# State-space layer: two heads side by side in the array, decay rows and sample rows laid out on 128 rows, state times C in four quarters

## The chip, the cores and the metric

One Trainium2 chip, one core. The metric is the device time of one execution in microseconds, the median of three runs. All matrices lie in HBM as float32. The engines are TensorE (PE in the profile; PEld is its weight load), VectorE (DVE), ScalarE (ACT), GpSimd (POOL) and SyncE (SP), which issues the DMAs.

## The reference, cut to what matters

Four decoder layers (retention, state space, gated delta net, retention), each with a token mixer and an MLP, run over a prompt of 256 tokens and 8 samples of 4 tokens with the same weights: T = 288 columns in the kernel. The state-space mixer (32 heads of width 64, 8 groups of 4 heads, state width 128) is where most of the change lies:

```python
def _ssd(h, conv_buf, s0, w_in, conv_w, conv_b, dt_bias, a_log, d_skip, norm_w, w_out):
    z, xbc, dt = jnp.split(h @ w_in, [...], axis=-1)
    xbc, new_buf = _causal_conv(xbc, conv_buf, conv_w)
    xs, b_in, c_out = jnp.split(jax.nn.silu(xbc + conv_b), [...], axis=-1)
    dt = jax.nn.softplus(dt + dt_bias)
    log_a = dt * (-jnp.exp(a_log))
    y, s_new = _decay_scan(c_out, b_in, xs * dt[..., None], log_a, s0g)
    y = y + d_skip * xs
    ...
def _decay_scan(q, k, v, log_a, s0):
    ct = jnp.cumsum(log_a)
    decay = jnp.where(incl, jnp.exp(ct[..., :, None] - ct[..., None, :]), 0.0)
    scores = jnp.einsum('bctgn,bcsgn->bcgts', qc, kc)
    y_intra = jnp.einsum('bcgrts,bcsgrp->bctgrp', scores[:, :, :, None] * decay, vc)
    y_inter = jnp.einsum('btgn,bgrnp,bgrt->btgrp', q_c, S, jnp.exp(ct_c))
    S = S * jnp.exp(ct_c[..., -1]) + jnp.einsum('bsgn,bgrs,bsgrp->bgrnp', k_c, w_end, v_c)
```

`y_inter` of the samples is state times C: each of the 8 samples has a state of its own for each head. The retention and delta-net mixers use the same idea of a decay per head; their outputs are normed per token and head and turned back into the layout of features on rows.

## The kernel before, in words

Activations lie as features on 128 partitions by 288 columns. Every dense product (`dense`, lines 192 to 225) splits the weights and the activations into two float32r parts and runs three matmuls for each 128x128 weight tile and 288 columns (L222, L223, L224, into `psd`): 12,336 of the 16,248 matmuls. The weights come by DMA into `raw`, ScalarE casts them (`wh`, L207) and VectorE makes the rest (`wl`, L210).

A mixer is worked in four units (`units`, m = 0 to 3; in the state-space layer a unit is two groups, g = 0 and 1, of four heads each). Within a unit a generator, the chain (`scan` in the retention and state-space layers, `prep` and `loop` in the delta net), yields estimated waits in us, and `weave` fills each wait with blocks of dense products: the unit's gate, the projection of the next unit and the output product of an earlier one. `fin` of unit m-1 runs ahead of the chain of unit m. The Tile framework then orders each engine's instructions by its own estimates. Each engine works its list in order. PSUM tiles come from `self.ps`: tag "m" has three banks, tag "s" two.

In a state-space unit `scan` does the following:

- State times C (L1090 to L1109): for each group, 8 samples' states `S` are transposed two samples at a time on TensorE (`ps_sT`), copied by ScalarE (`sT`, two buffers), and each sample's masked C (`cm`, 32 columns) is multiplied with it into `yi`. The output block of a matmul is 32 rows: sample b of a pair goes to rows 32*(2*g+b), so group 0 uses rows 0 to 63 and group 1 rows 64 to 127, with 256 columns. The products of four pairs are summed in each block.
- The states are updated (`ps_up`, L1111 to L1128) and stored; `yis` (L1132) is `yi` scaled by the decay of each token, group by group.
- For each of the eight heads, in four pairs: a matmul spreads the head's cumulative decay over 128 rows (`ps_cbc`, L1142). Its operands are `e2`, a column of ones at two places, and `cts`, the decays as a high part on rows 0 to 31 and a remainder on rows 32 to 63: 64 rows contracted. ScalarE makes the decay factors (`Et`, three buffers, L1147 to L1149), VectorE multiplies them with the scores `gm` (L1151). Then come the head's two products, 256 and 128 columns, into 64 rows of `y` (64*r for head r of the pair, L1155 and L1156). After both heads: one matmul adds `yis` (64 rows contracted, both heads' 128 outputs), two add the samples' own part (`xds`, 32 rows contracted). All lines of the local helper `mm` have line 983 in the profile.

In the retention layers `fin` (L748) transposes `yt` back: for each of four blocks two full 128x128 transposes and one of the 32 sample rows (L756). In the delta net `prep` spreads decays in the same way from 64 rows (`ps_dif`, L1354), and `fin` (L1696) transposes, for each of four heads, two prompt blocks (L1702, L1703) and 32 rows of `on2`, the samples' result (L1704). `on2` is written in two halves of 64 rows by `sample` (L1586): heads 0 and 1 first, heads 2 and 3 later.

Of the kernel before, what the change touches and what calls it, by code (L numbers as in the profile page):

```python
# [35 lines left out]
def make_consts():  # L36
# [50 lines left out]
    gm[:, 128:160] = np.tile(c["ssd_tris"][:, 0:32], (4, 1))  # L87
# [36 lines left out]
class K:  # L124
# [422 lines left out]
    def retention(self, ctx, j, i):  # L547
# [61 lines left out]
        def scan(h):  # L609
# [138 lines left out]
        def fin(h, ah, al):  # L748
            u = units.pop(h)
            yt, sgs = u["yt"], u["sg"]  # L750
            for z in range(4):
# [4 lines left out]
                nc.tensor.transpose(ps[:, 256:288], yt[:32, 2, zs], self.ident[:32, :32])  # L756
# [164 lines left out]
    def ssd(self, ctx, j, i):  # L921
# [15 lines left out]
        e2 = cp.tile([64, 32], F32R, name="e2")  # L937
# [9 lines left out]
        A.copy(e2, istk[0:64])  # L947
# [26 lines left out]
        la = rp.tile([128, 3, 2, 32], F32, name="la")  # L974
        for d in range(2):
# [32 lines left out]
        mm(ps[:64, 0:128], la2[:, 0], tri)  # L1008
        mm(ps[:64, 128:256], la2[:, 1], tri)
        mm(ps[:64, 256:288], la2[0:32, 2], tris[:, 0:32])  # L1010
        cth = rp.tile([64, T], F32R, name="cth")
        cts = rp.tile([64, T], F32R, name="cts")
        A.copy(cth, ps[:64, 0:T])
        V.scalar_tensor_tensor(out=cts, in0=cth, scalar=self.sel[:64, 0:1], in1=ps[:64, 0:T], op0=ALU.mult, op1=ALU.add)
# [13 lines left out]
        def scan(m):  # L1028
# [61 lines left out]
            for g in range(2):  # L1090
# [8 lines left out]
                for bp in range(4):  # L1099
                    ps = self.ps("ps_sT", "s")  # L1100
                    for b in range(2):
                        for q in range(2):
                            PE.transpose(ps[:, (2 * b + q) * 128:(2 * b + q + 1) * 128], S[q][:, 2 * bp + b], self.ident)
                    sT = rp.tile([128, 2, 256], F32, name="sT", tag="sT", bufs=2)
                    A.copy(sT.rearrange("p a b -> p (a b)"), ps)
                    for b in range(2):
# [22 lines left out]
            yis = rp.tile([128, 256], F32, name="yis", tag="yis")  # L1129
            for g in range(2):  # L1130
# [671 lines left out]
```

## Time and profile before

| | us |
|---|---|
| median of three runs | 2324.92 (2324.84 to 2326.75) |
| the profiled execution's own time | 2332.37 |
| its span, first to last instruction | 2330.2 |
| PE busy / DVE busy / ACT busy / POOL busy | 2241.3 / 1565.0 / 1245.0 / 574.3 |
| mean granted TensorE clock | 0.965 of 2.4 GHz |
| HBM traffic | 394.87 MB, 169 GB/s |

The span divides as follows: retention to about 290 us, its MLP to 570, the state-space layer to 900, its MLP to 1150, the delta net to 1550, its MLP to 1780, the second retention to 2100, the last MLP to the end. A busy time of PE counts matmuls whose ends are modelled and that overlap in the array, so the distance from one matmul's start to the next one's start says what a matmul costs. Times in a timeline are us from the span's start. A tile's form such as `64*128` is the rows and columns of the array that a matmul uses, and what follows is its output. A float32 matmul runs as two passes, so one matmul of the program shows as x2; a float32r one and a transpose run as one.

### The profile page before, as it was taken

What the parts mean: (1) busy time and instruction counts of PE and PEld (TensorE: products, weight loads), DVE (VectorE), ACT (ScalarE), POOL (GpSimd) and SP (SyncE); (2) the same over time, 40 slices, a digit from 0 to 9 for tenths busy, and PEclk for the clock granted to TensorE, in tenths of its full rate; (3) what the DMA queues carried; (4) which work ended last, traced back from release to release, by engine and by line L of the source; (5) the groups of instructions that cost most, each with busy time, mean ns of one, the idle gap of its engine ahead of it and who ended that gap; (6) DMA issues with size and microseconds to landing.
All of it is one profiled execution on the core that took longest, in us unless ns stands there. A gap on an engine that the chain in (4) does not pass through costs nothing. (4 is left out here: it accounts for less than half of the span.)

```text
span 2330.2 us, 42937 instructions
## 1 busy us (share of the span) xinstructions
PE 2241.3 (96%) x16248; PEld 2045.3 (88%) x16248; DVE 1565.0 (67%) x3209; ACT 1245.0 (53%) x2825; POOL 574.3 (25%) x597
## 2 busy tenths in 40 slices
PE   9999997998999999999899999999999999999998
PEld 8888797998888888999888888789899888879998
DVE  6777774557887777555786685557675777766554
ACT  5444463544667665555466566366655444445454
POOL 2110012332331222333332121124443001003333
PEclk9999998999999999999899998789999999999999
DMA  6786754545445543554433342247865666754553
GB/s 202 262 260 220 239 162 136 169 151 156 125 132 173 165 134 112 180 169 155 146 120 98 108 129 85 84 122 220 253 206 166 211 238 222 262 208 154 168 166 111
DMA packets 406656, 394.87 MB, mean 169 GB/s; under 512 B 15569, under 2 KB 356154, under 8 KB 406354
## 3 DMA queue, kind: packets, MB, share of 16 engines
q1 hardware_dynamic: 406290, 391.88, 53.2%
q8 instruction: 127, 2.08, 0.4%
q14 instruction: 79, 0.65, 0.1%
q10 hardware_dynamic: 96, 0.20, 0.0%
q0 software_dynamic: 64, 0.07, 0.0%
HBM read 333.41 MB, written 58.69 MB: 168 GB/s over the span
## 5 line engine op out<-in xcount | busy, mean ns | idle before, releaser
L207 ACT CAST wh<-raw 128x512 fp32r<-128x512 f32 x1024 | 627.0, 619 | 706.8 <-PE psd L223 649.3
L210 DVE TENSOR_TENSOR wl<-raw,wh 128x512 fp32r<-128x512 f32 x1024 | 741.6, 731 | 334.9 <-ACT wh L207 320.2
L222 PE MATMUL psd<-xh,wh 128*128 128x288 f32 x2576 | 782.1, 304 | 6.6 <-ACT xh L297 4.6
L223 PE MATMUL psd<-xl,wh 128*128 128x288 f32 x2576 | 776.2, 302 | 3.0 <-DVE xl L298 2.4
L224 PE MATMUL psd<-xh,wl 128*128 128x288 f32 x2576 | 774.4, 301 | 3.3 <-DVE wl L210 3.2
L222 PEld LDWEIGHTS psd<-xh,wh 128*128 128x128 f32 x2576 | 490.3, 191 | 28.7 <-issue 10.7
L223 PEld LDWEIGHTS psd<-xl,wh 128*128 128x128 f32 x2576 | 493.9, 192 | 19.2 <-issue 9.8
L224 PEld LDWEIGHTS psd<-xh,wl 128*128 128x128 f32 x2576 | 492.8, 191 | 13.5 <-DVE wl L210 5.6
L222 PE MATMUL psd<-ah,wh 128*128 128x288 f32 x1536 | 466.9, 304 | 24.5 <-ACT wh L207 11.3
L224 PE MATMUL psd<-ah,wl 128*128 128x288 f32 x1536 | 463.2, 302 | 4.2 <-DVE wl L210 4.1
L223 PE MATMUL psd<-al,wh 128*128 128x288 f32 x1536 | 463.9, 302 | 0.0
L222 PEld LDWEIGHTS psd<-ah,wh 128*128 128x128 f32 x1536 | 295.3, 192 | 35.5 <-ACT wh L207 19.5
L224 PEld LDWEIGHTS psd<-ah,wl 128*128 128x128 f32 x1536 | 296.6, 193 | 10.4 <-DVE wl L210 6.0
L223 PEld LDWEIGHTS psd<-al,wh 128*128 128x128 f32 x1536 | 296.1, 193 | 8.4 <-issue 6.5
L482 POOL TENSOR_TENSOR x<-x,dn 128x288 f32<-128x288 f32 x120 | 149.1, 1243 | 250.2 <-DVE dn L480 250.2
L463 POOL TENSOR_TENSOR a<-v 128x288 f32<-128x288 f32 x128 | 108.9, 851 | 271.9 <-ACT v L462 267.2
L725 DVE SCALAR_TENSOR_TENSOR S<-S,ps_up 128x512 f32<-128x512 f32 x128 | 83.4, 684 | 58.5 <-PE ps_up L724 49.9
L826 DVE SCALAR_TENSOR_TENSOR cacc<-U,cw,cacc 128x312 f32<-128x312 f32 x192 | 105.0, 552 | 10.1 <-ACT cacc L821 8.1
L465 DVE TENSOR_TENSOR al<-a,ah 128x288 fp32r<-128x288 f32 x128 | 59.4, 464 | 73.5 <-POOL a L463 69.4
L263 POOL TENSOR_TENSOR rs_y<-ms,mhalf 128x3 f32<-128x3 f32 (+3 forms) x37 | 36.5, 989 | 292.2 <-DVE ms L741 226.9
L802 POOL COPY U<-cb 128x24 f32<-128x24 f32 x64 | 35.0, 552 | 224.4 <-DVE cacc L826 106.7
L480 DVE TENSOR_TENSOR dn<-psd,rb 128x288 f32<-128x288 f32 x128 | 58.2, 454 | 40.5 <-PE psd L224 40.4
(498 smaller groups left out, 2658.6 us busy)
## 6 DMA issues: line engine op xcount, KB each, us to landing
raw<-mlp_w_up SPq DMA_DIRECT2D x64, 1024.0 KB
raw<-mlp_w_down SPq DMA_DIRECT2D x64, 1024.0 KB
S<-state_ret SPq DMA_DIRECT2D x64, 512.0 KB
raw<-ret_w_in SPq DMA_DIRECT2D x32, 1024.0 KB
s_ret<-S SPq DMA_DIRECT2D x64, 512.0 KB
raw<-ssd_w_in SPq DMA_DIRECT2D x24, 1024.0 KB
raw<-gdn_w_in SPq DMA_DIRECT2D x24, 1024.0 KB
raw<-ret_w_in SPq DMA_DIRECT2D x32, 512.0 KB
```

Of the source, the lines that this page charges most:

```text
L207: self.last_cast = nc.scalar.copy(wh, src)
L210: nc.vector.tensor_tensor(out=wl, in0=src, in1=wh, op=ALU.subtract)
L222: nc.tensor.matmul(po, lhsT=hs[k][:, os], rhs=xh[k], start=(k == 0), stop=False)
L223: nc.tensor.matmul(po, lhsT=hs[k][:, os], rhs=xl[k], start=False, stop=False)
L224: self.last_mm = nc.tensor.matmul(po, lhsT=ls[k][:, os], rhs=xh[k], start=False, stop=(k == kt - 1))
L263: self.nc.gpsimd.tensor_tensor(out=y[rows], in0=ms[rows], in1=self.mhalf[rows].broadcast_to([rows.stop - rows.start, n]), op=ALU.pow)
L463: nc.gpsimd.tensor_tensor(out=a, in0=v, in1=v, op=ALU.mult)
L465: nc.vector.tensor_tensor(out=al[o], in0=a, in1=ah[o], op=ALU.subtract)
L480: nc.vector.tensor_tensor(out=t, in0=ps, in1=rb2, op=ALU.mult)
L482: e.tensor_tensor(out=self.x[o], in0=self.x[o], in1=t, op=ALU.add)
L725: nc.vector.scalar_tensor_tensor(out=S[:, b, z], in0=S[:, b, z], scalar=C["g4"][h], in1=up, op0=ALU.mult, op1=ALU.add)
L826: nc.vector.scalar_tensor_tensor(out=acc[:, 0:n], in0=u, scalar=wk, in1=acc[:, 0:n], op0=ALU.mult, op1=ALU.add)
```

## The change

It changes seven things.

1. `e2`, `la`, `cts` and `cth` of the state-space layer have four copies on 128 rows where two lay on 64. `e2` is halved, so that the sum is the same. The matmul `ps_cbc` now contracts 128 rows.
2. The same for `gd`, `e2`, `cth` and `cts` of the delta net (`ps_dif`).
3. State times C runs on four samples at a time: sample b of four goes to rows 32*b, group g to columns 256*g. Two pairs are transposed and copied, then four matmuls follow. Each block sums two products.
4. `yis` is one VectorE instruction on 128x512 in place of two on 64x256, and the four row blocks are summed in the last matmul, which contracts 128 rows with four stacked identities.
5. The samples' own part contracts 128 rows: the tokens lie on the rows four times already, and the mask is divided by 4.
6. A pair's decays (`decays(pr)`) are issued one pair ahead of its products, `Et` has four buffers, and the products of the two heads alternate: 256 columns of both, 128 columns of both, the samples' part of both, the states' part of both.
7. The sample transposes at the end of retention (L756) and of the delta net (L1704) become matmuls over all 128 rows with 32 columns of the identity. In retention GpSimd clears the tile's third block first.

```diff
-    gm[:, 128:160] = np.tile(c["ssd_tris"][:, 0:32], (4, 1))
+    gm[:, 128:160] = np.tile(c["ssd_tris"][:, 0:32], (4, 1)) / 4.0
...
+            nc.gpsimd.memset(yt[:, 2], 0.0)
...
-                nc.tensor.transpose(ps[:, 256:288], yt[:32, 2, zs], self.ident[:32, :32])
+                nc.tensor.matmul(ps[:, 256:288], lhsT=yt[:, 2, zs], rhs=self.ident[:, :32], start=True, stop=True)
...
-        A.copy(e2, istk[0:64])
+        A.mul(e2, istk, 0.5)
...
-        for d in range(2):
+        for d in range(4):
             V.tensor_tensor(out=la[:, :, d], in0=dt, in1=bcm(nea, 3), op=ALU.mult)
...
-                for bp in range(4):
...
-                    for b in range(2):
-                        c = 32 * (2 * g + b)
-                        PE.matmul(yi[c:c + 32, 0:256], lhsT=cm[:, 2 * bp + b], rhs=sT[:, b], start=bp == 0, stop=bp == 3)
-                    yield YS[2]
+                for bq in range(2):
+                    sTs = []
+                    for bp in (2 * bq, 2 * bq + 1):
...
+                    yield 2 * YS[2]
+                    for b in range(4):
+                        PE.matmul(yi[32 * b:32 * b + 32, 256 * g:256 * g + 256], lhsT=cm[:, 4 * bq + b],
+                                  rhs=sTs[b // 2][:, b % 2], start=bq == 0, stop=bq == 1)
...
+            yv = []
+            P = decays(0)
+            yield YS[4]
+            for pr in range(4):
+                nxt = decays(pr + 1) if pr < 3 else None
+                if nxt:
+                    yield YS[4]
+
+                y = self.ps("ps_y")
+                hd = [(y[64 * r:64 * r + 64], slice(64 * (2 * pr + r), 64 * (2 * pr + r) + 64), P[r]) for r in range(2)]
+                for ys, cs, p in hd:
+                    mm(ys[:, 0:256], xdt[:, 0, cs], p[:, 160:416], True, False)
+                for ys, cs, p in hd:
+                    mm(ys[:, 128:256], xdt[:, 1, cs], p[:, 0:128], False, True)
+                for ys, cs, p in hd:
+                    mm(ys[:, 256:288], xds[:, cs], p[:, 128:160], True, False)
+                for ys, cs, p in hd:
+                    mm(ys[:, 256:288], yis[:, cs], istk, False, True)
...
-                PE.transpose(ps[:, 256:288], on[2][hp], ident[hp, hp])
+                PE.matmul(ps[:, 256:288], lhsT=on[2], rhs=ident[:, hp], start=True, stop=True)
```

The order of TensorE's list moves at three places that matter. In the rows a line number of the changed kernel is higher by the lines added above it (L984 is the helper L983, L1713 is L1704).

First, a pair of heads in the first state-space unit, before (`psd` is a dense product, its numbers tell tiles apart):

```order
L983 MATMUL ps_cbc<-cts,e_4177 128x288
L224 MATMUL psd<-xh_6834,wl 128x288
L983 MATMUL ps_y<-Et,xdt 64x256
L983 MATMUL ps_y<-Et,xdt 64x128
L222 MATMUL psd<-xh_6840,wh 128x288
L223 MATMUL psd<-xl_6841,wh 128x288
L983 MATMUL ps_y<-Et,xdt 64x256
L983 MATMUL ps_y<-Et,xdt 64x128
L983 MATMUL ps_y<-c_ssd_istk,yis 128x32
L983 MATMUL ps_y<-Et,xds 64x32 x2
```

and a pair of the same unit in the changed kernel:

```order
L222 MATMUL psd<-xh_6864,wh 128x288
L223 MATMUL psd<-xl_6865,wh 128x288
L224 MATMUL psd<-xh_6864,wl 128x288
L984 MATMUL ps_y<-Et,xdt 64x256 x2
L984 MATMUL ps_y<-Et,xdt 64x128 x2
L984 MATMUL ps_y<-Et,xds 64x32 x2
L984 MATMUL ps_y<-c_ssd_istk,yis 64x32 x2
L222 MATMUL psd<-xh_6822,wh 128x288
```

Dense products stood between the two heads of the pair; now both heads' products follow each other, the samples' parts too.

Second, a pair in the fourth unit of the changed kernel:

```order
L984 MATMUL ps_y<-Et,xdt 64x256
L984 MATMUL ps_cbc<-cts,e_4181 128x288
L224 MATMUL psd<-ah_10027,wl 128x288
L222 MATMUL psd<-ah_10028,wh 128x288
L223 MATMUL psd<-al_10032,wh 128x288
L224 MATMUL psd<-ah_10028,wl 128x288
L222 MATMUL psd<-ah_10029,wh 128x288
L223 MATMUL psd<-al_10033,wh 128x288
L984 MATMUL ps_y<-Et,xdt 64x256
L984 MATMUL ps_y<-Et,xdt 64x128 x2
```

Here the first head's 256 columns stand alone, and the second head's follow after a `ps_cbc` and dense products. Of the 16 pairs of the layer nine are in one piece, and seven are split like this one or by the products `ps_ps`.

Third, the end of the delta net (`fin` of its last unit), where `on` with a number is `on2`, before:

```order
L1702 MATMUL ps_oT<-c_ident,on 128x128
L1703 MATMUL ps_oT<-c_ident,on 128x128
L1704 MATMUL ps_oT<-c_ident,on_18602 128x32 x2
L1702 MATMUL ps_oT<-c_ident,on 128x128
L1703 MATMUL ps_oT<-c_ident,on 128x128
L222 MATMUL psd<-ah_18729,wh 128x288 x3
L223 MATMUL psd<-al_18733,wh 128x288
L224 MATMUL psd<-ah_18729,wl 128x288
L222 MATMUL psd<-ah_18730,wh 128x288
L1704 MATMUL ps_oT<-c_ident,on_18602 128x32 x2
```

and in the changed kernel:

```order
L1711 MATMUL ps_oT<-c_ident,on 128x128 x2
L1712 MATMUL ps_oT<-c_ident,on 128x128 x2
L1711 MATMUL ps_oT<-c_ident,on 128x128
L1712 MATMUL ps_oT<-c_ident,on 128x128
L1713 MATMUL ps_oT<-c_ident,on_18622 128x32 x3
L1711 MATMUL ps_oT<-c_ident,on 128x128
L1712 MATMUL ps_oT<-c_ident,on 128x128
L1713 MATMUL ps_oT<-c_ident,on_18622 128x32
L222 MATMUL psd<-ah_18749,wh 128x288 x3
```

Two heads' sample rows were turned ahead of the other two's, with dense products between; now three heads' stand together, and the fourth head's three matmuls and the dense products come after them. The three other units end in the same way.

## Rows read from the trace of the kernel before

**Rows 1.** Busy time by stretch: start:end, us, then PE, PEld, DVE, ACT, POOL; granted clock; DMA

```profile
0.00:290.00 290.00, 284.12 (x1798) 234.78 (x1799) 210.52 (x423) 129.82 (x248) 34.15 (x43) 0.99 0.74 236
...
590.00:900.00 310.00, 302.63 (x2113) 257.00 (x2112) 242.03 (x509) 205.33 (x570) 75.59 (x72) 1.00 0.48 143
...
1150.00:1550.00 400.00, 372.92 (x3234) 336.04 (x3234) 266.38 (x722) 225.94 (x608) 86.06 (x116) 0.89 0.32 101
```

**Rows 2.** Timeline of PE at a lone `ps_cbc`: start us, us, then the instructions

```profile
639.89 0.29 PE L224 MATMUL psd<-xh,wl 128*128 128x288 f32 x1
640.11 0.40 PE L983 MATMUL ps_cbc<-cts,e 64*128 64x288 f32 x1
640.44 0.40 PE L222 MATMUL psd<-xh,wh 128*128 128x288 f32 x1
640.68 0.29 PE L223 MATMUL psd<-xl,wh 128*128 128x288 f32 x1
640.81 0.29 PE L224 MATMUL psd<-xh,wl 128*128 128x288 f32 x1
```

**Rows 3.** Timeline of PE, second head of a pair and the samples' parts

```profile
643.15 0.86 PE L983 MATMUL ps_y<-Et,xdt 128*64 128x256 f32 x4
643.94 0.41 PE L983 MATMUL ps_y<-c_ssd_istk,yis 64*128 64x32 f32 x2
644.28 0.30 PE L983 MATMUL ps_y<-Et,xds 32*64 32x32 f32 x4
644.51 0.40 PE L222 MATMUL psd<-xh,wh 128*128 128x288 f32 x1
644.75 0.30 PE L223 MATMUL psd<-xl,wh 128*128 128x288 f32 x1
```

**Rows 4.** Timeline of PE, a pair whose two heads follow each other

```profile
719.22 0.88 PE L983 MATMUL ps_y<-Et,xdt 128*64 128x256 f32 x8
720.03 0.41 PE L983 MATMUL ps_y<-c_ssd_istk,yis 64*128 64x32 f32 x2
```

**Rows 5.** Timeline of PE, state times C for two samples

```profile
618.39 0.62 PE L1108 MATMUL ps_yi<-sT,cm 128*32 128x256 f32 x4
618.95 0.40 PE L223 MATMUL psd<-xl,wh 128*128 128x288 f32 x1
619.19 0.29 PE L224 MATMUL psd<-xh,wl 128*128 128x288 f32 x1
```

**Rows 6.** Timeline of PE in retention, four blocks of 32 rows, 512 columns

```profile
60.10 1.06 PE L716 MATMUL ps_yi<-S,qm 128*32 128x512 f32 x8
61.10 0.50 PE L724 MATMUL ps_up<-vst,km 128*128 128x512 f32 x1
```

**Rows 7.** Timeline of PE, 32 columns over the whole array

```profile
611.42 0.31 PE L983 MATMUL ps_g<-Ct,rep 128*128 128x32 f32 x2
611.57 0.90 PE L983 MATMUL ps_g<-Ct,Bt 128*128 128x256 f32 x4
```

**Rows 8.** Timeline of PE, transposes at the end of a retention unit

```profile
105.18 0.33 PE L754 MATMUL ps_yT<-c_ident,yt 128*128 128x128 f32 x1
...
105.55 0.24 PE L756 MATMUL ps_yT<-c_ident,yt 32*128 32x32 f32 x1
105.72 0.33 PE L754 MATMUL ps_yT<-c_ident,yt 128*128 128x128 f32 x1
```

**Rows 9.** Busy time in the pair stretches 635:667, 711:741, 797:830, 870:896, summed

```profile
sum 121.00, PE 120.99 PEld 95.07 DVE 89.40 ACT 89.77 POOL 21.67; mean PE 30.25 PEld 23.77 DVE 22.35 ACT 22.44 POOL 5.42
```

**Rows 10.** Timeline of PE at the end of a delta-net unit, the sample transposes

```profile
1261.55 0.25 PE L1704 MATMUL ps_oT<-c_ident,on 32*128 32x32 f32 x2
...
1265.66 0.25 PE L1704 MATMUL ps_oT<-c_ident,on 32*128 32x32 f32 x2 [0.16 <-ACT on L1586]
```

**Rows 11.** One line's instructions: the decay copies of the state-space layer

```profile
L976 DVE TENSOR_TENSOR la<-sp_r,nea x2: 247/248/249, 573.5 to 573.7; 128x96 f32<-128x96 f32 x2
```

**Rows 12.** Busy time by stretch at the start of the state-space layer

```profile
580.00:590.00 10.00, 7.71 (x34) 7.27 (x35) 8.71 (x22) 6.13 (x14) 5.59 (x6) 0.52 0.14 45
```

More of the change, by code (lines that the diff above doesn't have):

```diff
@@ L936, in ssd @@
                                              ("ssd_tri", "ssd_trs", "ssd_tris", "ssd_trss", "ssd_istk", "ssd_mask"))
-        e2 = cp.tile([64, 32], F32R, name="e2")
+        e2 = cp.tile([128, 32], F32R, name="e2")
         dsk = cp.tile([128, 16], F32, name="dsk")
@@ L1007, in ssd @@
         ps = self.ps("ps_cT")
[L1008 to L1014, printed above, removed]
+        mm(ps[:, 0:128], la2[:, 0], tri)
+        mm(ps[:, 128:256], la2[:, 1], tri)
+        mm(ps[:, 256:288], la2[0:32, 2], tris[:, 0:32])
+        cth = self.tmp.tile([128, T], F32R, name="cth", tag="t288", bufs=3)
+        cts = rp.tile([128, T], F32R, name="cts")
+        A.copy(cth, ps[:, 0:T])
+        V.scalar_tensor_tensor(out=cts, in0=cth, scalar=self.sel[:, 0:1], in1=ps[:, 0:T], op0=ALU.mult, op1=ALU.add)
         units = {}
@@ L1128, in scan, with decays @@
                     yield YS[3]
-            yis = rp.tile([128, 256], F32, name="yis", tag="yis")
-            for g in range(2):
-                gs = slice(64 * g, 64 * g + 64)
-                V.tensor_tensor(out=yis[gs].rearrange("p (h d) -> p h d", d=64),
-                                in0=yi[gs, 0:256].rearrange("p (h d) -> p h d", d=64),
-                                in1=bc3(ect[gs, 8 * m + 4 * g:8 * m + 4 * g + 4], 64), op=ALU.mult)
-            yv = []
-            for pr in range(4):
-                g = pr // 2
-                y = self.ps("ps_y")
+            yis = rp.tile([128, 512], F32, name="yis", tag="yis")
+            V.tensor_tensor(out=yis.rearrange("p (h d) -> p h d", d=64), in0=yi.rearrange("p (h d) -> p h d", d=64),
+                            in1=bc3(ect[:, hs], 64), op=ALU.mult)
+            def decays(pr):
                 Ps = []
                 for r in range(2):
-                    hl = 2 * pr + r
-                    h = 8 * m + hl
+                    h = 8 * m + 2 * pr + r
                     bc = self.ps("ps_cbc", "s")
-                    mm(bc[:, 0:T], e2[:, h:h + 1].broadcast_to([64, 128]), cts)
-                    Et = rp.tile([128, 416], F32, name="Et", tag="Et", bufs=3)
+                    mm(bc[:, 0:T], e2[:, h:h + 1].broadcast_to([128, 128]), cts)
+                    Et = rp.tile([128, 416], F32, name="Et", tag="Et", bufs=4)
                     for (o, n, src, gi) in ((160, 128, 0, 0), (0, 128, 128, 1), (128, 32, 256, 2)):
@@ L1237, in gdn @@
         i4, s4 = m4[:, 0], m4[:, 1]
[L1238 to L1240 removed]
+        istk = cp.tile([128, 16], F32, name="istk")
+        nc.sync.dma_start(istk, I["ssd_istk"][:, 0:16])
+        e2 = cp.tile([128, 16], F32R, name="e2")
         dtb = self.rowbc(cp, "dtb", I["gdn_dt_bias"][j], 16)
@@ L1283, in gdn @@
         V.tensor_tensor(out=g, in0=sp.rearrange("p (g h) -> p g h", g=3), in1=bcm(nea, 3), op=ALU.mult)
-        gd = small("gd", 2, 2, 32)
+        gd = small("gd", 2, 4, 32)
         V.memset(gd, 0.0)
-        for d in range(2):
+        for d in range(4):
             V.tensor_copy(gd[:, :, d, 0:16], g[:, 0:2])
```

48 lines of the change are left out of this document (19 added, 29 removed).

## The prediction

> **What bounds the kernel now.** I read the busy time by stretch first. TensorE is busy for 302.6 of the 310 us of the state-space layer, for 284.1 of 290 in the first retention and for 372.9 of 400 in the delta net [rows 1]. Its clock is granted in full in the state-space layer (1.00, which is 2.4 GHz) and at 0.89 in the delta net, where it waits more often. So in the first two stages a saved us of TensorE is nearly a us of the kernel as long as VectorE (242.0 of 310) and ScalarE (205.3) keep up; in the delta net it is less.
>
> Next I read the timeline of TensorE where a matmul uses fewer than 128 rows or columns of the array. In a run of dense products the starts lie 0.13 us apart (the last two rows of [rows 2]). At a lone `ps_cbc`, which uses 64 rows, 0.22 us pass from the start of the dense product before it, 0.33 us to the next one, and 0.24 us to the one after that [rows 2]. That is 0.79 us where two dense products alone take 0.26: the matmul costs 0.53 us, though it streams the same 288 columns as a dense product does in 0.13. So entering and leaving a narrower form of the array costs about 0.40 us here, and each change between two narrow forms shows again: 0.79, 0.34 and 0.23 us for the second head's products, the states' part and the samples' part, which use 128x64, 64x128 and 32x64 of the array, and 0.24 us after it [rows 3].
>
> **The change part by part, in TensorE's time.** The counts come from the code and from the timeline of the layer.
>
> *Decay broadcast.* 32 times 0.53 us become 32 times 0.13, since the new form is that of a dense product in float32r: 12.8 us saved. Thirteen of them touch another narrow group and share a change with it, so I take off 1.5.
>
> *Pairs of heads.* Thirteen of the 16 pairs have dense products between the heads. The first head's group costs 0.22 + 0.79 + 0.24 - 0.26 = 0.99 us, the second with the two small parts 0.22 + 0.79 + 0.34 + 0.23 + 0.24 - 0.26 = 1.56 [rows 2, 3]: 2.55 a pair. In three pairs the heads happen to follow each other, and both heads' eight passes take 0.81 us to the next start, where one head's four take 0.79 [rows 3, 4]: side by side, the second head is nearly free. Such a pair costs 1.58. In all 13 x 2.55 + 3 x 1.58 = 37.9 us. In the changed kernel a pair in one piece enters once (0.22), runs eight passes (0.81), then eight short ones in the same form instead of six in two forms (the last four of today take 0.23 [rows 3], I take 0.3), and leaves (0.24): 1.31 us after the 0.26. Seven of the pairs are split in TensorE's new list. A split one runs the first head's two long passes alone, with an entry and an exit more; it can't cost more than a whole group of today more (0.99) nor less than nothing, and I take 0.7, as it has half of that group's passes and both changes. So 16 x 1.31 + 7 x 0.7 = 25.9, and 12.0 us are saved.
>
> *State times C.* A group for two samples takes 0.56 us to the next start and costs 0.22 + 0.56 + 0.24 - 0.26 = 0.76 [rows 2, 5]. There are 32 groups in 25 pieces; a second group in a piece pays no change and adds about 0.43. That makes 18 x 0.76 + 7 x 1.19 = 22.0 us. Four blocks of 32 rows at once are seen in retention: eight passes of 512 columns in 1.00 us [rows 6], twice the time of today's 256 columns for two blocks, so four blocks cost what two do. Then 16 groups cost 12.2, and 9.8 us are saved.
>
> Together the state-space layer loses 12.8 - 1.5 + 12.0 + 9.8 = 33 us of TensorE's time.
>
> *How much of it is kept.* In the four stretches of the pairs, 121.0 us long, TensorE is busy throughout; ScalarE has 89.8 us of work there and VectorE 89.4 [rows 9]. With 23 us less for TensorE 98 us are left, and both others would be at 92%. That can be done but leaves little room for their waits. Kept are all 33 us at most, and at least the 10 of state times C, which lies where both have more room. I take 28, nearer the upper end, since decays are now issued a pair ahead and `Et` has a fourth buffer.
>
> *Sample transposes of retention.* One block takes 0.54 us from first transpose to first transpose [rows 8], of which the 32-row one and its two changes take what is left after two full transposes of 0.11 us. A float32 matmul over the whole array with 32 columns takes 0.15 us from its first pass to the next start [rows 7], or up to 0.22 if its first pass waits for the weights too. So a block comes to 0.44 at most, and 32 blocks save 3.2 us or a little more. I take 3. The cleared tile is POOL work, eight times; POOL is busy for 34.2 of the 290 us [rows 1], and what stands behind the memset in its list has slack of many us. If it were not covered, it would cost a wait of `yt` of that instruction's length, eight times.
>
> The Trainium skill, "TensorEngine Tiling (Array Packing)", section "When to Use Tiling", speaks against this edit: a contraction over 32 rows is to be given a quarter of the array's rows, so that four fit side by side. By it, as an estimate, the transpose in a quarter of the array would be worth a quarter of the padded 0.22 us, the padding would lose 0.16 us for each of 48 blocks in retention and delta net, and the sum below would be some 13 us smaller. The row decides for me: only one such transpose stands there at a time, and what it costs is the two changes.
>
> *Delta net.* Eight pairs of `ps_dif` lose a narrow form at about 0.40 us each (the nearest rows are [rows 2]), 3.2 us; 16 sample transposes save at most 1.6. Against this stands a new wait: each head's matmul reads all 128 rows of `on2`, so heads 0 and 1 now wait for the half that belongs to heads 2 and 3, 4.1 us later in the first unit [rows 10]. Three heads then hold all three "m" banks of PSUM, and the fourth head's transposes, the convolution's transposes and the next unit's `ps_qk` queue behind them. The cost lies between nothing (dense products fill the time) and four times 4.1 = 16.4 us. I take 4, mostly from the last unit, which has no dense products left to fill with, and set it against the 4.8 saved: nothing.
>
> *The start.* Two more decay copies of 0.25 us each [rows 11] lie on the way to the first unit, and two small ones in the delta net: 0.5 to 1 us lost; I take 0.5. The other edits (masks divided by 4, `e2` halved, a single `yis` in place of two halves) change values or join instructions and cost nothing.
>
> **Sum.** 28 + 3 + 0 - 0.5 = about 31 us. Against the profiled execution's 2332.4 that is 2301; the median of the runs lies 7.5 us lower, so I predict 2294 us.
>
> **The rivals.**
>
> *ScalarE and VectorE bind.* If the four pair stretches don't shrink, 9 of 10 us from state times C and 3 from retention remain: 2325 - 12 = 2313 us. For it: 92% is needed of two engines that work in order, and they have 74% today [rows 9]. Against it: VectorE was busy for 8.71 of 10 us in a stretch where TensorE had waits [rows 12], so it can run well above its 74%. Chance 0.13.
>
> *The wait for `on2`.* If all of the 4.1 us in four units lands on the end, 12 of it beyond my 4: 2306 us. Against it: dense products stand beside the fins of three units. Chance 0.10.
>
> *Slower: the clock falls.* At the start of the layer, from 580 to 590 us, after waits of TensorE, its grant is 0.52, about the lower level of 1.2 GHz, while it is busy for 7.71 us [rows 12]. If ScalarE holds the pair stretches at 121 us while TensorE has 98 us of work, TensorE gets waits there too, and may be granted the lower level for part of them. Work done at the lower level takes twice as long. The first 23 us of that fill the idle time, the next 12 eat what the rival of ScalarE still saves; so it decides from about a third of the 98 us on. With half of them, 2313 + 49 - 23 = 2339 us. Against it: the grant is 1.00 in the whole layer after its start [rows 1]. Chance 0.04.
>
> *The heads don't run side by side, or the new list costs elsewhere what it gains.* [Rows 4 and 6] speak against it; then within 0.2% of before. Chance 0.04.
>
> **How the numbers follow.** My case, 2283 to 2303 us, has 0.67, and 0.02 lies below it (everything kept and no new wait). 0.2% is 4.6 us, about what a measurement of this kernel can tell from no change. Faster by more: 0.67 + 0.02 + 0.13 + 0.10 = 0.92. Within it 0.04, slower 0.04. The range goes from 2280 (33 + 3 of TensorE's time and all of the delta net's 4.8 kept, with a few us of chance) to 2313, where ScalarE binds.
>
> **What would show it.** Right: no form narrower than 128 rows in the state-space pairs; the 32 `ps_cbc` 0.13 us apart from dense products; both heads' first passes within 0.02 us; the layer 25 to 30 us shorter at a granted clock of 1.00; ScalarE and VectorE at about 90% in the pair stretches. Wrong: new idle time of TensorE before `ps_y` behind ScalarE's `Et`, a granted clock below 1.00 there, or a delta net longer by over 5 us with TensorE waiting for `on2`.

## The result, and the profile after

| | before | after |
|---|---|---|
| median | 2324.88 (2321.26 to 2326.75, 4 runs) | 2292.15 (2290.19 to 2295.40, 4 runs) |
| ratio, 95% interval | | 0.9862 [0.9845, 0.9880] |
| profiled execution / its span | 2332.37 / 2330.2 | 2290.19 / 2288.4 |
| mean granted clock | 0.965 | 0.973 |

The kernel became 32.7 us faster and takes 2292.15 us; 31 us and 2294 were predicted. The two profiled executions differ by 42, since that of before lies 7.5 us above its median and that of after 2 below. To see where the time went I cut the span at the first `v` (L462) of each MLP, which both kernels have:

| stretch, us | before | after | difference |
|---|---|---|---|
| start to first MLP (retention) | 327.4 | 326.8 | -0.6 |
| to second MLP (first MLP and state-space layer) | 598.1 | 572.1 | -26.0 |
| to third MLP (second MLP and delta net) | 639.2 | 627.2 | -12.0 |
| to fourth MLP (third MLP and second retention) | 549.1 | 545.9 | -3.2 |
| to the end | 216.4 | 216.4 | 0 |

Below, "the state-space stage" and "the delta-net stage" are the second and third of these. The busy time by stretch of the changed kernel, columns as in [rows 1]:

```profile
0.00:290.00 290.00, 281.78 (x1810) 234.40 (x1811) 208.88 (x423) 129.14 (x248) 36.25 (x47) 0.99 0.74 236
590.00:873.00 283.00, 274.40 (x2137) 246.36 (x2137) 238.84 (x503) 202.63 (x569) 76.79 (x72) 1.00 0.52 157
1125.00:1512.00 387.00, 356.07 (x3251) 324.47 (x3250) 268.03 (x725) 227.03 (x609) 85.55 (x116) 0.93 0.34 106
```

In the state-space layer TensorE has 274 us of work in place of 303, at the same full clock, and VectorE and ScalarE have what they had. In the delta net the mean granted clock is 0.93 in place of 0.89.

The timeline of TensorE at a whole pair of the changed kernel (compare [rows 3, 4]):

```profile
641.52 0.29 PE L224 MATMUL psd<-xh,wl 128*128 128x288 f32 x1
641.74 0.87 PE L984 MATMUL ps_y<-Et,xdt 128*64 128x256 f32 x8
642.44 0.26 PE L984 MATMUL ps_y<-Et,xds 128*64 128x32 f32 x4
642.53 0.29 PE L984 MATMUL ps_y<-c_ssd_istk,yis 128*64 128x32 f32 x4
642.75 0.40 PE L222 MATMUL psd<-xh,wh 128*128 128x288 f32 x1
642.99 0.29 PE L223 MATMUL psd<-xl,wh 128*128 128x288 f32 x1
```

One entry (0.22), sixteen passes in one form (1.01), one exit (0.24): 1.20 us more than two dense products, where a pair in two groups took 2.55 in the kernel before. A split pair's lone first half, and its second half:

```profile
636.77 0.30 PE L223 MATMUL psd<-xl,wh 128*128 128x288 f32 x1
636.99 0.65 PE L984 MATMUL ps_y<-Et,xdt 128*64 128x256 f32 x2
637.57 0.40 PE L224 MATMUL psd<-xh,wl 128*128 128x288 f32 x1
...
638.17 0.65 PE L984 MATMUL ps_y<-Et,xdt 128*64 128x256 f32 x4
```

A lone half costs 0.78 us here, two changes of form for two passes. I counted every narrow group of the state-space layer in this way, from the start of the dense product ahead of it to the start of the second behind it, less 0.26:

| groups, us in all | predicted | in the trace after |
|---|---|---|
| pairs, whole or second halves | 16 x 1.31 = 21.0 | 16, 19.9 |
| lone first halves | 7 x 0.7 = 4.9 | 7, 6.1 |
| `ps_cbc`, now a dense form | 32 x 0.13 = 4.2 | 32 x 0.15 = 4.8 |
| `ps_yi` | 16 x 0.76 = 12.2 | 16, 18.4 |
| all narrow groups of the layer, unchanged ones too, without `ps_cbc` after | | 56.3 (89.0 before) |

Where a group's neighbour is no dense product (`ps_up` and `ps_sT` around `ps_yi`), its cost counted in this way is up to 0.4 us off, as that neighbour's own starts are not 0.13 us apart.

The pairs come out at 26.0 us where 25.9 stood in the sum. `ps_yi` doesn't. A group that costs what was predicted, and one that doesn't, with what ScalarE does ahead of it:

```profile
612.11 0.64 PE L1112 MATMUL ps_yi<-sT,cm 128*32 128x256 f32 x8
612.68 0.40 PE L222 MATMUL psd<-xh,wh 128*128 128x288 f32 x1
```

```profile
627.00 0.87 PE L1106 MATMUL ps_sT<-c_ident,S 128*128 128x128 f32 x6 [0.45 <-DMA S<-state_ssd]
...
627.68 1.05 ACT L1108 COPY sT<-ps_sT 128x512 f32<-128x512 f32 x2
...
628.29 1.11 PE L1112 MATMUL ps_yi<-sT,cm 128*32 128x256 f32 x8
...
628.78 0.14 PEld L1112 LDWEIGHTS ps_yi<-sT,cm 128*32 128x32 f32 x4 [0.34 <-ACT sT L1108]
```

At 612.11 all eight passes take 0.57 us to the next start, the same as four passes for two samples did [rows 5]. At 628.29 two samples run alone, the weight load of the other two waits 0.34 us for ScalarE's second copy, and these follow: 1.05 us from the first start to the next `ps_sT` at 629.34. From first start to next start the 16 groups take 13.8 us where 16 x 0.57 is 9.1, so 4.7 of the 6.2 us too many are time inside the groups; the rest is what stands beside them. Of the 16 groups, four stand 24 dense products behind their transposes and cost 0.70 to 0.87 us; of the twelve with 0 to 4 in between, the one at 612.11 costs 0.75, the others 1.05 to 1.66, and those with none are the dearest.

### The profile page after: what moved, and what is told of

It is laid out like the page before. It is cut to its first block, busy times and chain, and to the rows that moved or that the text cites. A ratio compares the mean times of both kernels' runs of the same rounds, so it can differ in the third digit from the quotient of the medians.

```text
span 2288.4 us, 43119 instructions
## 1 busy us (share of the span) xinstructions
PE 2192.8 (96%) x16328; PEld 2024.9 (88%) x16328; DVE 1561.3 (68%) x3209; ACT 1242.8 (54%) x2825; POOL 578.9 (25%) x605
## 5 line engine op out<-in xcount | busy, mean ns | idle before, releaser
L803 POOL COPY U<-cb 128x24 f32<-128x24 f32 x64 | 34.1, 538 | 222.0 <-DVE cacc L827 111.3
```

## The experiments

The kernels ran beside the kernel before on their chip, so ratios are to that. The stages come from each run's own trace. Four kernels with the same products in the state-space layer (the changed kernel, ssd_only, delta_fin_undone, st_four_buffers) have 572.1, 570.2, 570.9 and 571.7 us in the state-space stage, so it tells about 2 us apart, but only where the granted clock is alike: the stages have stretches at the lower level of 1.2 GHz, and these are not equally long in all traces. Dense products start 0.24 us apart there (the rows of delta_fin_undone) and 0.13 at the full clock, so, as an estimate, half of the time that TensorE is busy at the lower level is what the clock costs, if TensorE is the bound.

The time of a whole run follows the clock too. The 50 runs of the kernel before that were made beside the experiments go from 2314.66 us at a mean granted clock of 0.974 to 2336.07 at 0.963, and a straight line through them has 1.7 us for each 0.001. The first column brings each run to 0.970 with that line (an estimate) and takes the median. In brackets stands the time of the stage in which TensorE was busy at the lower level.

| kernel | at 0.970, us | state-space stage | delta-net stage |
|---|---|---|---|
| before | 2322 | 598.1 (22.7) | 639.2 (97.0) |
| changed | 2295 | 572.1 (23.2) | 627.2 (63.2) |
| ssd_only | 2296 | 570.2 (17.2) | 639.4 (101.9) |
| rest_only | 2321 | 596.0 (20.4) | 630.1 (69.4) |
| delta_fin_undone | 2295 | 570.9 (22.1) | 639.0 (96.1) |
| decay64 | 2300 | 575.9 (21.6) | 624.0 (59.0) |
| yi_by_two | 2295 | 572.9 (22.9) | 628.9 (67.4) |
| no_decays_ahead | 2296 | 572.7 (22.9) | 632.1 (80.0) |
| st_four_buffers | 2295 | 571.7 (21.5) | 618.6 (46.9) |
| yi_eight | 2300 | 578.6 (30.1) | 632.2 (80.2) |
| st_four_heads_reversed | 2291 | 562.2 (16.7) | 636.7 (86.9) |
| tails_padded | 2297 | 568.5 (16.0) | 628.0 (65.7) |
| all_together | 2292 | 574.2 (34.1) | 633.9 (81.8) |
| reversed_wide_tails | 2291 | 566.2 (16.8) | 635.2 (81.7) |

So at an equal clock the change is worth about 27 us, and the higher clock the other 6. No run undoes the alternating of the two heads, `yis` or the samples' part alone (points 4 to 6 of the change): what they are worth is read from the trace.

### Which layer the gain is in

ssd_only, the changed kernel with these taken back (and the delta net's `e2`, `gd`, `cth`, `cts` on 64 rows):

```
-nc.gpsimd.memset(yt[:, 2], 0.0)
...
-nc.tensor.matmul(ps[:, 256:288], lhsT=yt[:, 2, zs], rhs=self.ident[:, :32], ...)
+nc.tensor.transpose(ps[:, 256:288], yt[:32, 2, zs], self.ident[:32, :32])
...
-PE.matmul(ps[:, 256:288], lhsT=on[2], rhs=ident[:, hp], start=True, stop=True)
+PE.transpose(ps[:, 256:288], on[2][hp], ident[hp, hp])
```

> The changed kernel with the retention and delta-net edits taken back, so that only the state-space layer differs from the kernel before. Theory (the state-space layer holds nearly all of the gain, the retention edits 3 us, the delta net nothing): about 2295 us, 28 to 30 below the kernel before. Rival (the 12 us by which the delta net of the changed kernel's trace is shorter are a gain of its edits): 2304 to 2307 us.

Measured: 2299.95 us, 0.9891 [0.9869, 0.9912]; state-space stage 570.2, delta-net stage 639.4, both retentions together 872.0 (after: 872.7).

rest_only, the kernel before with just those edits:

> The kernel before with only the retention and delta-net edits. Theory: 3 us of retention and nothing of the delta net, 2320 to 2323 us against 2325. Rival (the delta net gains 8 to 12): 2310 to 2314 us. If the wait for on2 costs what was taken off for it without the 4.8 us coming back: 2326 us.

Measured: 2321.08 us, 0.9989 [0.9974, 1.0005]; state-space stage 596.0, delta-net stage 630.1, both retentions 873.3 (before: 876.5).

By the medians the state-space layer alone gives 24 us (ssd_only against its kernel before), and 29 on top of the other edits (the changed kernel against rest_only); by its stage 26. The rest is in the delta net: its stage is 639 us without the edits, 627.2 and 630.1 with them. By the medians the rest is worth 3 to 8 us, and rest_only's interval still holds no change at all. rest_only's time lies where the theory had it, but not by its terms: the theory gave the delta net nothing. For retention the two pairs disagree: rest_only has 3 us less in the two stages than the kernel before, as predicted, but ssd_only has without the edits what the changed kernel has with them.

### Which delta-net edit, and how

delta_fin_undone, the changed kernel with one line as before:

```
-PE.matmul(ps[:, 256:288], lhsT=on[2], rhs=ident[:, hp], start=True, stop=True)
+PE.transpose(ps[:, 256:288], on[2][hp], ident[hp, hp])
```

> The changed kernel with the delta net's sample transposes as before (32 rows of on2 a head, no wait for the other half), its decay broadcast as changed. Theory of the prediction (16 transposes save 1.6 us at most, the wait costs 4): 1 to 3 us faster than the changed kernel, 2290 us. Rival 1 (the edit moves TensorE's list so that its clock is granted in full for longer, which is where the delta net's 10 us in the traces come from): 8 to 10 us slower, 2300 us, with a stretch of some 35 us at 0.50 in the last unit. Rival 2 (the gain is the decay broadcast's): the same time as the changed kernel, 2292 us.

Measured: 2302.21 us, 0.9897 [0.9874, 0.9921]; delta-net stage 639.0 in place of 627.2. Rival 1 came true, in time (10 us by the medians, 8 by the ratios, whose intervals overlap at the edge) and in the trace. The timeline of the last unit in this run (edit undone), two dense products at the lower level among it, then the busy time there:

```profile
1453.99 3.63 PE L1279 MATMUL ps_kS<-qk,St 128*128 128x8 f32 x32
...
1459.25 0.45 PE L224 MATMUL psd<-ah,wl 128*128 128x288 f32 x1
1459.49 0.45 PE L222 MATMUL psd<-ah,wh 128*128 128x288 f32 x1
...
1463.07 3.58 PE L1279 MATMUL ps_kS<-qk,St 128*128 128x8 f32 x16
1467.13 3.42 PE L1279 MATMUL ps_kS<-qk,St 128*128 128x8 f32 x16
```

```profile
1454.00:1459.00 5.00, 5.00 (x42) 4.66 (x41) 2.20 (x8) 1.02 (x3) 0.00 (x0) 0.97 0.34 96
1459.00:1499.00 40.00, 40.00 (x343) 33.49 (x343) 9.35 (x26) 11.30 (x31) 0.78 (x2) 0.50 0.16 55
```

And in the changed kernel:

```profile
1444.61 3.64 PE L1279 MATMUL ps_kS<-qk,St 128*128 128x8 f32 x32
1459.27 3.74 PE L1279 MATMUL ps_kS<-qk,St 128*128 128x8 f32 x32
```

```profile
1459.00:1464.00 5.00, 5.00 (x40) 4.49 (x41) 1.25 (x6) 1.28 (x5) 0.00 (x0) 0.97 0.52 202
1464.00:1474.00 10.00, 10.00 (x68) 7.90 (x71) 4.67 (x14) 2.42 (x5) 0.00 (x0) 0.50 0.01 2
1474.00:1492.00 18.00, 18.00 (x297) 16.05 (x290) 6.43 (x17) 10.94 (x27) 2.49 (x4) 1.00 0.17 61
```

The samples' products `ps_kS` (32 matmuls of 8 columns) stand 9 us earlier in the list with the edit, and the two runs of them further apart. In both kernels the grant falls to the lower level (0.50, 1.2 GHz) behind the second run or, with the edit undone, the first; there two more runs of 16 follow at the lower level, and it stays for 40 us in place of 10, with TensorE busy all the time. Thirty us at half the clock are 15 us of work, but not all of it is gained: the changed kernel has 10 us at the lower level at the end of the unit, where this run has 3.

All three kernels with the old line (before, ssd_only and this one) have a stretch at the lower level of 30 us or more in the last unit, and in the eleven other traces the longest there is 14 us. That the line decides it is shown; why the list moves as it does, and that the place of `ps_kS` and not another part of the list holds the clock down, is what I read from the traces and was not tried by itself.

The line does not decide all of the 12 us between the two traces. In the third unit, too, this run has a stretch at the lower level that the changed kernel has not (this run first):

```profile
1383.00:1404.00 21.00, 21.00 (x157) 18.91 (x156) 5.72 (x14) 8.40 (x25) 0.00 (x0) 0.51 0.21 62
```

```profile
1398.00:1403.00 5.00, 5.00 (x26) 4.02 (x26) 0.76 (x2) 1.41 (x4) 0.00 (x0) 0.66 0.60 182
```

But seven of the eleven traces with the new line have that stretch of 20 us or more as well. The delta-net stage is 639.0 to 639.4 us with the old line and 618.6 to 636.7 with the new one, 629.7 on average: about 9 us less. At full clock, as an estimate (the stage less half of its time in brackets), it would be 588 to 591 with the old line and 592 to 596 with the new one. So without the clock the new line gains nothing and may cost the 4 us that the prediction took for the wait; the clock gives more back. The decay broadcast of the delta net shows nothing in the stage: 639.4 without it (ssd_only), 639.0 with it (this run).

### The parts of the state-space layer

decay64, the decay broadcast back on 64 rows:

```
-e2 = cp.tile([128, 32], F32R, name="e2")
+e2 = cp.tile([64, 32], F32R, name="e2")
...
-la = rp.tile([128, 3, 4, 32], F32, name="la")
+la = rp.tile([128, 3, 2, 32], F32, name="la")
...
```

> The changed kernel with the state-space decay broadcast back on 64 rows (e2, la and cts as before), all else as changed. Theory (32 ps_cbc at 0.53 us in place of 0.15, some of them sharing a change of form with another group): 8 to 12 us slower than the changed kernel, 2300 to 2304 us, and the ps_cbc cost 0.4 us more each in the timeline. Rival (ScalarE and VectorE bind in the pair stretches, so that TensorE's time there is free): at most 3 us slower, 2295 us.

Measured: 2301.19 us, 0.9885 [0.9855, 0.9916]; state-space stage 575.9. A lone `ps_cbc` costs 0.59 us (23 of them 13.6), so the array's side is as expected: all narrow groups come to 70.4 us in place of 56.3, or 9 more when the 4.8 of the dense `ps_cbc` are taken off. But the stage is only 3.8 us longer, and at 0.970 the kernel 5. The median lies in the theory's range, but four of its six runs had a clock of 0.970 or less, where three of the changed kernel's four had more. Neither theory: of this edit's TensorE time 4 to 5 of 9 us, give or take the 2 of a trace, reach the end once the other edits are in. The rest came out of waits: TensorE is idle for 24.6 us of the stage in place of 29.2.

yi_by_two, state times C issued behind each copy:

```
+                        for b in range(2):
+                            c = 32 * (2 * (bp % 2) + b)
+                            PE.matmul(yi[c:c + 32, ...], lhsT=cm[:, 2 * bp + b], rhs=sT[:, b], ...)
```

> The changed kernel with state times C issued two quarters at a time, behind each sT copy, as in the kernel before, with the layout of four quarters kept. Theory (in the trace of the changed kernel about half of the groups of four run as two and two anyway, behind the second sT copy, so the edit saved 3.6 us and not 9.8): 2 to 5 us slower than the changed kernel, 2294 to 2297 us. Rival, the prediction's own term (16 more groups at 0.76 us): 10 us slower, 2302 us.

Measured: 2291.69 us, 0.9861 [0.9837, 0.9885]; stage 572.9, `ps_yi` 18.8 us in 17 groups. The scheduler put nearly all of the products together again, whatever order the code issues them in, so this doesn't price the edit.

no_decays_ahead, each pair's decays right ahead of the pair:

```
-            P = decays(0)
-            yield YS[4]
             for pr in range(4):
-                nxt = decays(pr + 1) if pr < 3 else None
+                P = decays(pr)
...
```

> The changed kernel with each pair's decays issued right ahead of the pair, and not a pair ahead; Et keeps its four buffers. Theory of the prediction (the decays ahead and the fourth buffer are what lets the pairs keep their saving): TensorE waits for Et ahead of ps_y, the stage from the first MLP to the second 4 to 8 us longer than the changed kernel's 572.1 us, 11 split pairs in place of 7 among them. Rival (the order of the list follows from estimated times and the buffers, whatever order the code issues in): within 2 us, 570 to 574 us.

Measured: 2292.97 us, 0.9853 [0.9832, 0.9875]; stage 572.7. The time and the stage are the rival's, but not its reason: the list did change, to 12 lone halves in place of 7 (9.4 us against 6.1). TensorE's waits in the layer show none for `Et`; its idle time in the stage fell to 25.3 us from 29.2, which is where the longer list went. My reason for keeping 28 of 33 us, that decays are issued a pair ahead, falls; the fourth buffer, which I named beside it, was not taken away in any run.

### Why the groups of four cost more than predicted

st_four_buffers:

```
-sT = rp.tile([128, 2, 256], F32, name="sT", tag="sT", bufs=2)
+sT = rp.tile([128, 2, 256], F32, name="sT", tag="sT", bufs=4)
```

> The changed kernel with four buffers of sT in place of two (yis takes its turn in them, and lab a buffer of another pool, so that they fit); TensorE's list is the same. Theory (a group of four runs as two and two because the second sT copy has to wait for a buffer that the group before gives back): the ps_yi groups fall from 18.4 to about 12 us in all, and the time by as much, 2286 us. Rival (the second copy is late because ScalarE is behind in its list, whatever buffers there are): the groups stay at 17 to 18.4 us and the time at 2292.

Measured: 2289.28 us, 0.9858 [0.9831, 0.9885]; stage 571.7, the groups 18.4 us. Buffers are not it: the groups cost the same, and the 3 us of the median are the clock's (2295 us at 0.970, as the changed kernel). The two copies of 0.59 us run one after the other on ScalarE, and for most groups the list has only 0 to 4 dense products to pass that time.

yi_eight, with those buffers all eight samples' products together, held in the list behind a dense block:

```
...
+                yield 4.0
+                with tc.issue_after(self.last_mm.ins):
+                  for bq in range(2):
+                    for b in range(4):
+                        PE.matmul(yi[32 * b:32 * b + 32, ...], rhs=sTs[2 * bq + b // 2][:, b % 2], ...)
```

> The changed kernel with four sT buffers, and all eight products of a group of heads' state times C issued together, behind the four sT copies and, where the list allows it, behind a block of dense products (four of the eight groups then have 24 to 48 of them ahead, the four others none). Theory (a ps_yi group costs 0.7 us where its copies are done, and 1.05 to 1.66 us where it stands 0 to 4 dense products behind its transposes and waits for ScalarE): the four groups with dense products ahead cost 1.2 to 1.4 us for all eight samples, the four others 2.2 to 2.6, 14 to 16 us in all against 18.4, and the stage from the first MLP to the second is 2 to 4 us shorter than with the four buffers alone (571.7 us). Rival (the price is the array's, whatever the copies do): 2.0 us or more in all eight, 18 us in all.

Measured: 2304.06 us, 0.9896 [0.9874, 0.9918]; stage 578.6. The theory of the price holds where the copies are done: 1.30 us for each of five groups that stand 24 or more dense products behind them. The three without cost 1.48 to 1.68, less than expected, and all eight 11.2 us in place of 18.4. The timeline of one of the five:

```profile
619.26 1.07 PE L1114 MATMUL ps_yi<-sT,cm 128*32 128x256 f32 x16
620.26 0.73 PE L984 MATMUL ps_up<-bm,xwt 128*128 128x512 f32 x2
```

The time does not follow. The 7 us went in the same layer to the lone halves: the list now splits 12 pairs, and they cost 13.4 us against 6.1. So the narrow groups are no cheaper in all, and the stage is 6.9 us longer than with the four buffers alone: TensorE is idle for 2.4 us more, as it now waits for the decays, which it hardly did (0.6 us in the changed kernel), and it is busy for 8.6 us more at the lower level, an estimated 4. The waits of TensorE there:

```profile
PE ps_y L984 <- DVE Et L1150: 3.1, 3, 1.9
```

### A better version

st_four_heads_reversed, with four buffers, the second head's products first:

```
-hd = [(...) for r in range(2)]
+hd = [(...) for r in (1, 0)]
```

> As the one with four sT buffers, and in each pair the second head's products are issued ahead of the first head's, so that no pair is split in TensorE's list. Theory (seven split pairs cost 0.87 us each): no lone 64-column group is left, 6 us less than with the four buffers alone, 2280 us. Rival (the first head's product now waits for the second head's Et, so that TensorE gets waits there, or ScalarE binds): no gain, 2286 us.

Measured: 2287.30 us, 0.9841 [0.9815, 0.9867]; stage 562.2, 9.5 less than with the four buffers alone. No lone half is left, and all narrow groups together are 6 us less, as the theory has it; some 2.4 of the 9.5 are a higher clock in this trace (16.7 us at the lower level in place of 21.5). The delta-net stage took 636.7 us in this trace, 18 more than with the four buffers alone, 40 us more of it at the lower level. So the medians show 2 us, and at 0.970 it is 4 to 5.

tails_padded, the convolution's 35-column transposes widened:

```
-nc.tensor.transpose(ps[:35, a * 128:(a + 1) * 128], tails[a][1], self.ident)
+nc.tensor.transpose(ps[:, a * 128:(a + 1) * 128], tails[a][1], self.ident)
...
```

> The changed kernel with the convolution's 35-column transposes (ps_cs) widened to 128 columns in both layers that have a convolution. Theory (a narrow group costs two changes of form, 0.75 us a group in the trace, and not its columns): 12 to 16 groups at 0.4 to 0.6 us saved, 5 to 8 us faster than the changed kernel, 2285 to 2287 us. Rival (the wider output and the wider list cost what the changes give back): 2292 us.

Measured: 2297.84 us, 0.9878 [0.9852, 0.9904]; stage 568.5, 3.6 less. That is no gain of the edit: the 3.6 us are the clock's (16.0 us at the lower level in place of 23.2). Eight of these transposes between other full ones, in the changed kernel and in this one:

```profile
671.26 1.04 PE L845 MATMUL ps_cs<-c_ident,tl 128*35 128x128 f32 x8
672.14 0.62 PE L1040 MATMUL ps_xt<-c_ident,xs 128*128 128x128 f32 x4
```

```profile
668.63 1.07 PE L845 MATMUL ps_cs<-c_ident,tl 128*128 128x128 f32 x8
669.54 0.62 PE L1042 MATMUL ps_xt<-c_ident,xs 128*128 128x128 f32 x4
```

They take 0.88 us with 35 columns and 0.91 with 128, 0.11 a transpose in both. So the 35-column transposes pay no change of form, and the theory took their passes for it. The 4.5 us of lone `ps_cs` groups, which the sums of narrow groups hold, only go by another name when they are widened.

all_together, four buffers, eight products together, the second head first and the wide transposes:

> All that the runs so far point to at once: four sT buffers with eight products together, the second head's products first, and the 35-column transposes widened to 128 columns by reading the neighbours' columns along. Theory: the stage from the first MLP to the second 572.1 - 10 (no split pair) - 3.6 (wide transposes) - 3 (eight together) = 555 to 558 us, and the time 2270 to 2280 us, as the clock falls in the delta net. Rival (ScalarE and VectorE bind once TensorE has that much less work): not below 562 us, 2285 us.

Measured: 2297.48 us, 0.9875 [0.9855, 0.9894]; stage 574.2. The narrow groups fell to 40.3 us from 56.3, of which 4.5 are the widened transposes' change of name, and the stage grew by 2. By its numbers that is the rival, but its cause isn't shown. TensorE is idle for 34.8 us of the stage in place of 29.2, and it is busy at the lower level for 34.1 in place of 23.2, an estimated 5.5 us. The longest waits of TensorE from 570 to 892 us:

```profile
PE ps_sT L1108 <- DMA S<-state_ssd: 4.4, 3, 2.0
PE ps_cs L847 <- DVE tl L813: 4.0, 1, 4.0
PE psd L224 <- DVE wl L210: 2.4, 2, 1.9
```

The first was 2.3 us in the changed kernel, the second 2.7, and the third not there: a DMA and VectorE. At 0.970 the kernel is 3 us faster than the changed one, of 11 us of TensorE's time.

reversed_wide_tails, only the last two of these edits:

> The changed kernel with the second head's products issued first and the 35-column transposes widened to 128 columns by reading the neighbours' columns along; sT keeps its two buffers and the groups of four stand as in the changed kernel. Theory (these two leave the list as it is elsewhere, so their 9.5 and 3.6 us in the stage add up): the stage from the first MLP to the second 572.1 - 9.5 - 3.6 = 559 us, the time 2279 to 2283 us. Rival (with that much less work TensorE waits for others instead, as when the eight products stood together): not below 566 us, 2287 us or more.

Measured: 2293.06 us (2279.76 to 2299.77), 0.9850 [0.9819, 0.9881]; stage 566.2. The narrow groups fell by 8 us to 48.3, 3.5 without the widened transposes. Of the 5.9 us that the stage is shorter, some 3 are the clock's (16.8 us at the lower level in place of 23.2). Between theory and rival by the numbers; the part of the theory on the wide transposes falls. No version here beats the changed kernel by more than the intervals. At an equal clock the three with the second head first are 3 to 5 us faster.

## Why the prediction was right, and where not

**The whole**: 31 us predicted, 32.7 measured, but not by the same terms: the state-space stage gave 26.0 where 28 stood (with the same time at the lower level in both traces, 22.7 and 23.2 us), retention nothing that shows where 3 stood, and the delta net some 8 by the ratios (0.9897 to 0.9862), through the clock, where nothing stood. The errors cancel; that the sum came within 2 us is luck.

**Pairs**: right, 26.0 us against 25.9, whole pairs and second halves a little cheaper (1.24 on average against 1.31) and lone halves a little dearer (0.87 against 0.7). In a whole pair the first passes of the two heads start 7 ns apart, so they do run side by side.

**Decay broadcast**: right on the array (0.15 each after, 0.59 with 64 rows, 0.53 predicted); undone by itself it costs 4 to 5 us and not 11.3 (decay64).

**State times C**: the mis-sized term. "Sixteen groups at 0.76" holds for the array, as the first group and yi_eight show; what the sum left out is that a group of four needs two ScalarE copies one after the other, and that the list puts it right behind them. 18.4 us in place of 12.2, of which 4.7 are that wait and the rest the way of counting.

**What is kept**: TensorE's narrow work fell by 89.0 - 56.3 - 4.8 = 27.9 us, and the stage by 26.0. Nearly all was kept, a larger share than 28 of 33. The reason given, the decays ahead, is not it (no_decays_ahead). The engines are where the rival of ScalarE and VectorE put them: the pair stretches of the changed kernel, summed as in [rows 9]:

```profile
sum 78.00, PE 77.44 PEld 68.40 DVE 70.53 ACT 68.94 POOL 18.29; mean PE 19.36 PEld 17.10 DVE 17.63 ACT 17.23 POOL 4.57
```

90% and 88%, as predicted, and TensorE still hardly waits. The stretches are 78 us long and not 98, so some dense products stand elsewhere now. That rival was wrong for this change. What the next savings of TensorE's time return differs: the reversed heads' 6 us came back whole in the stage, decay64 has 4 to 5 of 9, all_together about 3 of 11. Which wait takes the rest is not shown.

**Retention**: 3 us were predicted; the changed kernel's first stretch is 0.6 shorter and its fourth 3.2, and ssd_only, without the edits, has 0.7 and 3.8. The fourth stretch's gain is the clock's: TensorE is busy at the lower level there for 15.5 us before, 10.2 after and 6.6 in ssd_only. Estimated at full clock the two stretches come to 866 us before and after and to 867 in ssd_only, so the term of 3 us doesn't show. The block itself is shorter than reckoned. The timeline of the changed kernel, next to [rows 8]:

```profile
106.17 0.27 PE L755 MATMUL ps_yT<-c_ident,yt 128*128 128x128 f32 x1
...
106.39 0.31 PE L757 MATMUL ps_yT<-c_ident,yt 128*128 128x32 f32 x2
106.53 0.31 PE L755 MATMUL ps_yT<-c_ident,yt 128*128 128x128 f32 x1
...
106.93 0.31 PE L755 MATMUL ps_yT<-c_ident,yt 128*128 128x128 f32 x1
```

0.36 to 0.40 us in place of 0.54, some 5 us over 32 blocks. Part of what it saved went into waits: TensorE's waits in the first 290 us are 8.1 us in place of 5.6, among them these, of which the first was 0.4 before and the second not there:

```profile
PE ps_st L325 <- DVE acc L293: 1.7, 1, 1.7
PE psd L223 <- DVE ssq L686: 0.9, 1, 0.9
```

The Trainium skill, "TensorEngine Tiling (Array Packing)", section "When to Use Tiling", would give a contraction over 32 rows a quarter of the array's rows. For a tile that stands alone the trace does not bear that out: the padded block takes 0.36 to 0.40 us and the quartered one 0.54. In the delta net the quartered form was 8 to 10 us slower, though there by the clock.

**Delta net**: the step that failed is the netting of 4.8 against 4, and the clock that it leaves out. Of the 4.8 nothing shows: the pairs of `ps_dif` cost 0.24 to 0.48 us each in place of 0.61 to 0.76, but the stage is the same without that edit. The wait was sized well: TensorE waits for `on2` 3.4 us in the changed kernel, 0.7 in the kernel before.

```profile
PE ps_oT L1713 <- ACT on L1595: 3.4, 4, 1.7
```

But an edit that moves the list also moves what stands beside it, and here the long stretch at the lower level in the last unit went with it (40 us before, 10 after). I had read the 0.89 of this layer and used it for nothing but a smaller return.

**Slower by the clock**: didn't come; the grant is 1.00 in the layer after its start, as before.

## What to carry to other kernels

Price a small matmul by starts, from the last dense product to the second one behind it. Here a lone `ps_cbc` on 64 rows pays about 0.4 us beside the 0.13 of its columns, and a lone half of a pair costs 0.87 for two passes, so join groups of one form, or pad a lone one to the whole array. But first look whether a group pays it: the 35-column transposes did not, 0.11 us each as the full ones.

Products that run side by side gain only if all their operands are there when the first starts (0.57 us for four samples, 1.05 where the second copy was late): look at what makes the last operand and how much work the list puts between.

Where the granted clock moves, compare neither whole times nor stages without it: 3.6 us of a stage here were the clock's and not the edit's.

## What the hardware showed that I had not expected

The clock stayed at its lower level for 40 us in which TensorE was busy for 40.0, in dense products with small ones among them. Over the runs the time follows the mean granted clock: the kernel before took 2314.66 us at 0.974 and 2336.07 at 0.963, so one kernel spreads over 21 us with no change in its list.

A transpose to 35 columns costs what a full one does, 0.11 us, and pays nothing for going in or out, while a head's products on 64 columns pay about 0.2 on either side together.

Four blocks of 32 columns take as long as two: 0.57 us for four samples and 0.56 for two [rows 5], and 1.00 for eight in one entry.
